# A twelve-pair part of an FFN down projection, computed from 7 block products in place of 8, in a hybrid encoder block on one Trainium2 core

## Chip, core and metric

One core of one Trainium2 chip runs the whole block (1 layer, 512 tokens, model width 2048, all float32). The metric is device time in microseconds of one execution, the median of a few runs.

## What is computed

Cut to what matters here: the second sub-layer, a SwiGLU FFN. Before it the reference runs a token-mixing sub-layer (projections, two attentions, gates, output projection) that the change does not touch.

```python
h = modulate(layer_norm(x), shift2, scale2)          # 512 x 2048
f = (silu(h @ w_ffn_gate) * (h @ w_ffn_up)) @ w_ffn_down   # width 5632, back to 2048
x = layer_norm_affine(DEEPNORM_ALPHA * x + gate2 * f, ln2_g, ln2_b)
```

## The kernel before

Every float32 matrix product is made of three passes of a rounded type: `split` (L94) makes a high part with a ScalarE cast (L97) and a low part with a VectorE subtraction (L98), and `mm3` (L77 to L81) issues high times high, high times low and low times high into one PSUM bank. A weight tile is loaded by SP with `load_raw` (L88, the DMA is L91, 512 KB) into one of 4 buffers named raw, and its two parts into one of 4 buffers each, wh and wl.

The FFN width of 5632 is worked on in 22 pairs of 128 columns. For 20 pairs the gate and up projections already use a 7-product scheme on 2 x 2 blocks (`strassen`, L1069; `weight_sums`, L1051, whose sums run on GpSimd at L1059 to L1061; `combine`, L1087, on VectorE). The hidden activations of a pair, 128 partitions by four blocks of 256 (two halves of the tokens times two column tiles), are multiplied at L1139 and stored to DRAM by `store_hid` (L1016, one DMA on ScalarE's queue).

Then comes the down projection, `down` (L1172): groups of 4 pairs (the fifth group has the rest, and the last 2 pairs are kept for the end). A group loads its hidden blocks (`load_hid`, L1106, SP, with a split at L1110 and L1111), and for each of four 512-wide column chunks takes 4 PSUM banks, one for each 128 tokens; for each pair it loads and splits the 256 x 512 piece of the weight, and issues 4 x 2 x 3 = 24 matmuls of 128x512. `drain` (L1156) then multiplies by gate2 (L1159) and adds to the residual (L1162, L1164), both on VectorE. The last two pairs (L1222 on) have gate2 multiplied into their weights on GpSimd (L1209) and are computed token tile by token tile with the final LayerNorm. In all the down projection is 22 x 96 = 2112 matmuls of 128x512.

A scheduler with a timeline of its own sets the order on every engine; DMAs of one queue start in that order, and an instruction that waits holds up what is behind it on its engine.

```python
for u in range(n):                                              # L1176
    hl = load_split(w_ffn_down, (g0 + u) * 256, 2, cc * 512, 512)
    for t in range(NT):
        for k in range(2):
            mm3(bb[t], hid[u].at(k, t), pair(hl, slice(None), k), u == 0 and k == 0, u == n - 1 and k == 1)
```

Of the kernel before, what the change touches and what calls it, by code (L numbers as in the profile page):

```python
# [46 lines left out]
def block_kernel(ctx: ExitStack, tc: tile.TileContext, x, c, w_ada, b_ada, w_in, b_gates, gqa_q_gain, gqa_k_gain,  # L47
# [1082 lines left out]

    for g in range(N_SPLIT, N_PAIR):
        eg = etile()
        bk = strassen(w_ffn_gate, 2 * g, "ssss")
        combine(eg, bk)
        nc.scalar.activation(out=eg, in_=eg, func=AF.Silu)
        bk = strassen(w_ffn_up, 2 * g, "ggtt", early_hid if g == N_PAIR - 1 else None)
        eu = sw.tile([P, 4, 256], F32, tag="eu", name="eu", bufs=1)
        combine(eu, bk)
        nc.vector.tensor_tensor(out=eg, in0=eg, in1=eu, op=ALU.mult)  # L1139
        store_hid(g, eg)  # L1140
    for u in range(3, GROUP):
        early_hid(u)

    pop("sop", "right")
    xp = push("xp", "right")
    x2 = [xp.tile([P, D], F32, name=f"x3_{t}") for t in range(NT)]
    fw = push("fw", "right")
    gate2 = fw.tile([P, D], F32, name="gate2")

    def load_residual(cc):  # L1150
        cs = slice(cc * 512, (cc + 1) * 512)
        nc.scalar.dma_start(out=gate2[:, cs], in_=rows_d[1][cs].partition_broadcast(P))
        for t in range(NT):
            nc.scalar.dma_start(out=x2[t][:, cs], in_=x2_d[t][:, cs])

    def drain(ps, t, cc, first_):  # L1156
        cs = slice(cc * 512, (cc + 1) * 512)
        tmp = fw.tile([P, 512], F32, tag="tmp", name="dtmp", bufs=3)
        nc.vector.tensor_tensor(out=tmp, in0=ps, in1=gate2[:, cs], op=ALU.mult)  # L1159
        v = x2[t][:, cs]  # L1160
        if first_:
            nc.vector.scalar_tensor_tensor(out=v, in0=v, scalar=ALPHA, in1=tmp, op0=ALU.mult, op1=ALU.add)  # L1162
        else:
            nc.vector.tensor_tensor(out=v, in0=v, in1=tmp, op=ALU.add)  # L1164

    turn8 = [0]

    def dbank():
        turn8[0] += 1
        return bank("ssssgtgt"[(turn8[0] - 1) % 8])  # L1170

    def down(g0, hid, first_, extra=None):  # L1172
        n = len(hid)
        for cc in range(4):
# [1 line left out]
            for u in range(n):  # L1176
                hl = load_split(w_ffn_down, (g0 + u) * 256, 2, cc * 512, 512)
                if first_ and u == 2:
                    load_residual(cc)
                for t in range(NT):  # L1180
                    for k in range(2):
                        mm3(bb[t], hid[u].at(k, t), pair(hl, slice(None), k), u == 0 and k == 0, u == n - 1 and k == 1)
            if extra is not None:
                extra(cc)
            for t in range(NT):
                drain(bb[t], t, cc, first_)

    g0 = 0
    for gi in range(4):
        hid = first_hid if gi == 0 else [load_hid(g0 + i, *hid_slot(4 * (gi % 2) + i)) for i in range(GROUP)]  # L1190
        down(g0, hid, gi == 0)
        g0 += GROUP
    pop("sw", "left")
    hp = push("hp", "left")

    def hp_hid(g):
        return load_hid(g, hp.tile([P, 4, 256], F32R, tag="hh", name="hh", bufs=6), hp.tile([P, 4, 256], F32R, tag="hl", name="hl", bufs=6))
# [5 lines left out]
    wslots = slots(a_pool, "A")[1] + slots(m0, "M")[1]

    def load_last(cc):
        for u in range(N_LAST):
            raw, v = load_raw(w_ffn_down, (gl + u) * 256, 2, cc * 512, 512)
            for k in range(2):
                nc.gpsimd.tensor_tensor(out=v[:, k, :], in0=v[:, k, :], in1=gate2[:, cc * 512:(cc + 1) * 512], op=ALU.mult)  # L1209
                h, l = wslots[cc * 4 + 2 * u + k]  # L1210
                nc.scalar.copy(out=h, in_=v[:, k, :])
                nc.vector.tensor_tensor(out=l, in0=v[:, k, :], in1=h, op=ALU.subtract)
                wl[cc, 2 * u + k] = (h, l)

    down(g0, hid, False, load_last)

    g2 = [hp.tile([P, 512], F32, tag="hh", name="g2", bufs=6) for _ in range(4)]
    b2 = [hp.tile([P, 512], F32, tag="hl", name="b2", bufs=6) for _ in range(4)]
    for j in range(4):
        nc.scalar.dma_start(out=g2[j], in_=ln2_g[0, j * 512:(j + 1) * 512].partition_broadcast(P))  # L1220
        nc.scalar.dma_start(out=b2[j], in_=ln2_b[0, j * 512:(j + 1) * 512].partition_broadcast(P))
# [54 lines left out]
```

## Time and profile before

| | |
|---|---|
| median of 3 runs | 2676.41 us (2674.88 to 2678.2) |
| the profiled execution | 2677.23 us, its span 2675.4 us |
| TensorE busy | 2599.7 us, 97% |
| VectorE, ScalarE, GpSimd busy | 1850.6, 1053.3, 1289.9 us |
| moved by DMA | 456.11 MB, 170 GB/s over the span |
| the down projection's matmuls | from 2185.24 to 2664.15 us of the span |

The span is what the trace covers; the rows are of this one execution. A busy TensorE says that matmuls were in flight, so the number of matmuls in a stretch is the better measure of its pace.

### The profile page before, as it was taken

The page shows a single profiled execution, that of the slowest core. Times are in us where ns is not written, and L with a number is a line of the kernel's source. Part 1 is how long each engine was busy: PE and PEld are TensorE (multiplying, and loading weights), DVE is VectorE, ACT ScalarE, POOL GpSimd, SP SyncE. Part 2 cuts the span into 40 slices and gives each one's busy share as a digit, 9 for nine tenths or more (in the row PEclk, how much of TensorE's full clock was granted, in tenths as well). Part 3 has the DMA queues.
Part 4 walks back from the last instruction along what each step waited for, and adds up shares of the span by engine and source line. Part 5 has one row for each costly group of instructions (what it writes and reads, how often), then busy time and mean ns, then how long its engine had stood idle before and what let it go on. Part 6 is the DMA issues. An engine that isn't in the chain of part 4 may idle for free.

```text
span 2675.4 us, 40191 instructions
## 1 busy us (share of the span) xinstructions
PE 2599.7 (97%) x15563; PEld 2319.2 (87%) x15563; DVE 1850.6 (69%) x2184; ACT 1053.3 (39%) x1525; POOL 1289.9 (48%) x1093
## 2 busy tenths in 40 slices
PE   6999999999989999999899999999999999999998
PEld 5778888788978888887899999999999998888886
DVE  8996688775678644576777777677676655445566
ACT  5542433332344533345644444444444432212321
POOL 4638778785755011021368767777776720000023
PEclk8999999999999999999999999999999999999999
DMA  9977577776744444667763333333333364334442
GB/s 349 295 224 240 165 219 236 241 248 192 212 140 134 127 148 142 225 231 240 229 193 119 115 122 119 118 120 119 111 124 122 111 213 157 115 108 132 150 126 87
DMA packets 330799, 456.11 MB, mean 170 GB/s; under 512 B 19656, under 2 KB 208480, under 8 KB 330096
## 3 DMA queue, kind: packets, MB, share of 16 engines
q1 hardware_dynamic: 307840, 414.77, 49.3%
q10 hardware_dynamic: 22768, 38.78, 4.1%
q8 instruction: 122, 2.00, 0.3%
q14 instruction: 69, 0.57, 0.1%
HBM read 418.87 MB, written 34.62 MB: 170 GB/s over the span
## 4 chain that ended last, share of the span: by engine, by line
PE 83%; POOL 5%; DVE 5%; DMA 3%; issue 2%; ACT 1%; POOLq 0%; SPq 0%; ACTq 0%; DVEq 0%
PE ps_s L81 16%; PE ps_s L80 16%; PE ps_s L79 16%; PE ps_g L80 7%; PE ps_g L79 7%; PE ps_g L81 7%; PE ps_t L80 4%; PE ps_t L79 4%; PE ps_t L81 4%; POOL acc L232 1%; DVE wl L98 1%; DMA braw<-in_w_ada_dram 1%; POOL tmp L228 1%; PE ps_t L584 1%; DVE acc L222 1%
## 5 line engine op out<-in xcount | busy, mean ns | idle before, releaser
L98 DVE TENSOR_TENSOR wl<-raw,wh 128x1024 fp32r<-128x1024 f32 (+2 forms) x342 | 456.9, 1340 | 319.2 <-ACT wh L97 317.6
L97 ACT CAST wh<-raw 128x1024 fp32r<-128x1024 f32 (+2 forms) x342 | 345.8, 1014 | 656.0 <-PE ps_s L81 280.3
L98 DVE TENSOR_TENSOR wl<-tt,wh 128x1024 fp32r<-128x1024 f32 x160 | 237.1, 1482 | 174.9 <-ACT wh L97 174.8
L1059 POOL TENSOR_TENSOR tt<-raw 128x512 f32<-128x512 f32 x160 | 245.8, 1537 | 197.1 <-DMA raw<-in_w_ffn_up_dram 69.5
L232 POOL TENSOR_TENSOR acc<-acc,tmp 128x512 f32<-128x512 f32 (+1 forms) x214 | 297.1, 1389 | 77.1 <-ACT tmp L230 64.6
L97 ACT CAST wh<-tt 128x1024 fp32r<-128x1024 f32 x160 | 167.9, 1049 | 305.9 <-PE ps_s L80 142.8
L1057 DVE TENSOR_TENSOR lr<-raw,hr 128x768 fp32r<-128x768 f32 x160 | 214.8, 1343 | 41.7 <-ACT hr L1056 40.6
L1209 POOL TENSOR_TENSOR raw<-raw,gate 128x512 f32<-128x512 f32 x16 | 25.2, 1600 | 401.0 <-DMA raw<-in_w_ffn_down_dram 400.5
L228 POOL TENSOR_SCALAR tmp<-braw,csil 128x512 f32<-128x512 f32 x112 | 135.4, 1211 | 119.7 <-DMA braw<-in_w_ada_dram 116.6
L1056 ACT CAST hr<-raw 128x768 fp32r<-128x768 f32 x160 | 133.7, 836 | 147.3 <-PE ps_t L80 70.4
L1061 POOL TENSOR_TENSOR tt<-raw,tt 128x256 f32<-128x256 f32 x160 | 173.5, 1085 | 11.9
L1060 POOL TENSOR_TENSOR tt<-raw,tt 128x256 f32<-128x256 f32 x160 | 165.9, 1037 | 11.9
L79 PE MATMUL ps_g<-hTh,wh 128*128 128x512 f32 x384 | 151.8, 396 | 0.0
L81 PE MATMUL ps_g<-hTh,wl 128*128 128x512 f32 x384 | 150.4, 392 | 0.0
L80 PE MATMUL ps_g<-hTl,wh 128*128 128x512 f32 x384 | 150.1, 391 | 0.0
L222 DVE SCALAR_TENSOR_TENSOR acc<-braw,csil,acc 128x512 f32<-128x512 f32 x112 | 113.4, 1012 | 43.3 <-DMA braw<-in_w_ada_dram 42.6
L79 PE MATMUL ps_s<-wh,hTh 128*128 128x512 f32 (+1 forms) x384 | 138.1, 361 | 0.0
L80 PE MATMUL ps_s<-wl,hTh 128*128 128x512 f32 (+1 forms) x384 | 137.5, 358 | 0.0
L81 PE MATMUL ps_s<-wh,hTl 128*128 128x512 f32 (+1 forms) x384 | 137.2, 358 | 0.0
L80 PE MATMUL ps_g<-sl,wh 128*128 128x256 f32 x480 | 135.8, 283 | 0.0
L80 PE MATMUL ps_s<-sl,wh 128*128 128x256 f32 x480 | 135.8, 283 | 0.0
L81 PE MATMUL ps_s<-sh,wl 128*128 128x256 f32 x480 | 135.5, 283 | 0.2 <-DVE wl L98 0.2
(437 smaller groups left out, 8315.2 us busy)
## 6 DMA issues: line engine op xcount, KB each, us to landing
braw<-in_w_ada_dram SPq DMA_DIRECT2D x128, 512.0 KB, 4.2
raw<-in_w_in_dram SPq DMA_DIRECT2D x96, 512.0 KB, 5.0
raw<-in_w_ffn_gate_dram SPq DMA_DIRECT2D x96, 512.0 KB, 3.6
raw<-in_w_ffn_up_dram SPq DMA_DIRECT2D x96, 512.0 KB, 3.6
raw<-in_w_ffn_down_dram SPq DMA_DIRECT2D x88, 512.0 KB, 3.7
raw<-in_w_out_dram SPq DMA_DIRECT2D x64, 512.0 KB, 4.1
lraw<-in_w_ada_dram SPq DMA_DIRECT2D x56, 512.0 KB, 5.5
braw<-in_w_in_dram SPq DMA_DIRECT2D x24, 512.0 KB, 5.2
```

The source lines that it names most:

```text
L79: nc.tensor.matmul(ps, lhsT=ah, rhs=bh, start=start, stop=False)
L80: nc.tensor.matmul(ps, lhsT=ah, rhs=bl, start=False, stop=False)
L81: nc.tensor.matmul(ps, lhsT=al, rhs=bh, start=False, stop=stop)
L97: nc.scalar.copy(out=h[:, :n], in_=src)
L98: nc.vector.tensor_tensor(out=l[:, :n], in0=src, in1=h[:, :n], op=ALU.subtract)
L222: nc.vector.scalar_tensor_tensor(out=acc[:, :n], in0=v[:, k, :], scalar=col, in1=acc[:, :n], op0=ALU.mult, op1=ALU.add)
L228: nc.gpsimd.tensor_scalar(out=dst[:, :n], in0=v[:, k, :], scalar1=col, scalar2=1.0, op0=ALU.mult, op1=ALU.mult)
L232: nc.gpsimd.tensor_tensor(out=acc2[:, :n], in0=acc2[:, :n], in1=dst[:, :n], op=ALU.add)
L1057: nc.vector.tensor_tensor(out=lr, in0=b[:, :, 1:4, :], in1=hr, op=ALU.subtract)
L1059: nc.gpsimd.tensor_tensor(out=t[:, :, 0:2, :], in0=b[:, :, 0:1, :].broadcast_to([P, 2, 2, P]), in1=b[:, :, 1:3, :], op=ALU.subtract)
L1060: nc.gpsimd.tensor_tensor(out=t[:, :, 2, :], in0=b[:, :, 2, :], in1=t[:, :, 0, :], op=ALU.subtract)
L1061: nc.gpsimd.tensor_tensor(out=t[:, :, 3, :], in0=b[:, :, 3, :], in1=t[:, :, 2, :], op=ALU.subtract)
```

## The change

For 12 of the 22 pairs (2 to 13) the product of hidden blocks and weight blocks is made from 7 block products. The 2 x 2 blocks are: token half by column tile of the pair for the activations, column tile of the pair by 1024-column half of the output for the weights. Each of the 7 products is 256 tokens by 128 by 1024. They are made in two sets: set 1 has 3 products, set 2 has 4, and each set runs over the 12 pairs once for each 512-column quarter c of a half. So a pass over one pair (a unit here) is 3 x 2 x 3 = 18 matmuls in set 1 and 24 in set 2, all 128x512.

- Hidden sums (`hidden_sums`): when a pair's activations are ready, four GpSimd operations of 128x256 make the sums, and 6 DMAs on ScalarE's queue store the blocks into `set1_d` and `set2_d` (before: 1 DMA).
- Set tiles: `need1` and `need2` load 384 KB or 512 KB of a pair into a half tile, and split it into one of 12 ring tiles. During the second quarter of set 1 the tile that was used last is handed on to set 2, and in the second quarter of set 2 to the plain pairs.
- Weights: each unit loads its blocks with 2 DMAs on SP (768 KB in set 1, 1024 KB in set 2), adds 256 KB more from DRAM with one accumulating DMA issued by GpSimd, makes 1 (set 1) or 2 (set 2) sums of 128x512 on VectorE, and splits 1536 or 2048 columns. Two half tiles, called a and b here, hold a unit's weights; half tiles are the 4 raw buffers and, once the up projection's tiles are gone, 4 new ones named tp, in turn.
- Results: after each quarter VectorE and ScalarE add the banks into the four token tiles of the sum; set 1 takes 6 banks a quarter, set 2 all 8. `convert` then multiplies by gate2 (GpSimd) and adds the residual, loaded again from DRAM (VectorE, 128x1024).
- The other 10 pairs run as before, in two groups of 4 and the 2 last; their tiles come from the ring and the half tiles.

```diff
+    def hidden_sums(g, eg, e):
+        nc.gpsimd.tensor_tensor(out=e[:, 0], in0=eg[:, 1], in1=eg[:, 2], op=ALU.subtract)
...
+        nc.scalar.dma_start(out=set1_d[g][:, 0:2, :], in_=e[:, 0:2])
+        nc.scalar.dma_start(out=set1_d[g][:, 2, :], in_=eg[:, 3])
+        for b, (t, k) in enumerate(((eg, 0), (e, 2), (eg, 2), (e, 3))):
+            nc.scalar.dma_start(out=set2_d[g][:, b, :], in_=t[:, k])
...
+    def half_tile():
+        place[1] += 1
+        if extra_tiles and place[1] % 2:
+            return extra_tiles[0].tile([P, 1024], F32, tag="tp", name="tp", bufs=4)
+        return raw_tile()
+
+    def load_set(arr, g, n):
+        v = half_tile()[:, :n * 256].rearrange("p (b n) -> p b n", b=n)
+        nc.sync.dma_start(out=v, in_=arr[g])
+        tl = ring_tile((n, g))
+        nc.scalar.copy(out=tl[:, 0:n, 0:256], in_=v)
+        nc.vector.tensor_tensor(out=tl[:, 0:n, 256:512], in0=v, in1=tl[:, 0:n, 0:256], op=ALU.subtract)
+        return tl
...
+    def weights1(g, c):
+        a, b = half_tile(), half_tile()
+        av, bv = a.rearrange("p (b n) -> p b n", b=2), b[:, :512]
+        nc.sync.dma_start(out=av, in_=w_rows(g, 0, c))
+        nc.sync.dma_start(out=bv, in_=w_rows(g, 1, c)[:, 1, :])
+        nc.gpsimd.dma_start(out=av[:, 1], in_=w_rows(g, 0, c)[:, 0, :], accum_op=ALU.add)
+        nc.vector.tensor_tensor(out=bv, in0=bv, in1=av[:, 1], op=ALU.add)
+        ah, al = split(a, 1024)
+        bh, bl = split(bv, 512)
+        return ((2, (ah[:, :512], al[:, :512])), (1, (bh[:, :512], bl[:, :512])), (0, (ah[:, 512:], al[:, 512:])))
+
+    def weights2(g, c):
...
+        nc.sync.dma_start(out=bv, in_=w_rows(g, 0, c))
+        nc.sync.dma_start(out=av, in_=w_rows(g, 1, c))
+        nc.gpsimd.dma_start(out=bv[:, 1], in_=w_rows(g, 1, c)[:, 1, :], accum_op=ALU.add)
+        nc.vector.tensor_tensor(out=bv[:, 0], in0=bv[:, 0], in1=av[:, 0], op=ALU.add)
+        nc.vector.tensor_tensor(out=bv[:, 0], in0=bv[:, 0], in1=bv[:, 1], op=ALU.add)
+        ah, al = split(a, 1024)
+        bh, bl = split(b, 1024)
...
+    def products(pairs, sets, weights, c, step):
+        bk = None
+        for u, g in enumerate(pairs):
+            ws = weights(g, c)
+            if bk is None:
+                bk = [dbank() for _ in range(2 * len(ws))]
+            step(u, False)
+            for j, (b, w) in enumerate(ws):
+                for i in range(2):
+                    mm3(bk[2 * j + i], block(sets[g], b, i), w, u == 0, u == len(pairs) - 1)
+            step(u, True)
+        return bk
...
+            for i in range(2):
+                add(nc.vector, z(0, 1, i, c), bk[i])
+            for i in range(2):
+                add(nc.vector, z(0, 0, i, c), bk[2 + i])
+            for i in range(2):
+                add(nc.vector, z(1, 0, i, c), bk[4 + i])
+                nc.vector.tensor_tensor(out=z(1, 1, i, c), in0=z(1, 1, i, c), in1=bk[4 + i], op=ALU.subtract)
+            for i in range(2):
+                add(nc.vector, z(1, 0, i, c), bk[6 + i])
```

How the built program's order moves, at two places. First SP's queue, the loads of the down projection. A group of the kernel before, hidden blocks of 4 pairs and then 16 weight pieces (L91):

```order
L1109 DMA raw<-hid_d 128x1024 x4
L91 DMA raw<-in_w_ffn_down_dram 128x2x512 x16
L1109 DMA raw<-hid_d 128x1024 x4
L91 DMA raw<-in_w_ffn_down_dram 128x2x512 x16
L1109 DMA raw<-hid_d 128x1024 x4
```

Some units of set 1, second quarter, in the changed program (L1203 loads a, L1204 b, L1129 is the set tile for set 2):

```order
L1129 DMA tp<-set_d 128x1024
L1204 DMA tp<-in_w_ffn_down_dram 128x512
L1203 DMA raw<-in_w_ffn_down_dram 128x2x512
L1129 DMA raw<-set_d 128x1024
L1204 DMA raw<-in_w_ffn_down_dram 128x512
L1203 DMA tp<-in_w_ffn_down_dram 128x2x512
L1129 DMA tp<-set_d 128x1024
L1204 DMA tp<-in_w_ffn_down_dram 128x512
L1203 DMA raw<-in_w_ffn_down_dram 128x2x512
```

Where a queue had one load for 24 matmuls, it now has three for 18, and raw and tp take turns.

Second VectorE, at the seam between the last up projection and the down projection. Before (L1090 to L1093 are `combine` of the last pair, L1139 its product):

```order
L98 TENSOR_TENSOR wl_22373<-raw_22370,wh_22372 128x1024
L98 TENSOR_TENSOR wl_22403<-raw_22400,wh_22402 128x1024
L98 TENSOR_TENSOR wl_22433<-raw_22430,wh_22432 128x1024
L1090 TENSOR_TENSOR eu_22342<-ps_g_22098,eu_22342 128x512
L1091 TENSOR_TENSOR eu_22342<-ps_g_22099,eu_22342 128x512
L1092 TENSOR_TENSOR eu_22342<-ps_g_22099,eu_22342 128x256
L1093 TENSOR_TENSOR eu_22342<-ps_t_22100,eu_22342 128x512
L1139 TENSOR_TENSOR eg_21863<-eg_21863,eu_22342 128x1024
```

In the changed program (L1206 is the sum in set 1, L1132 a set tile's low part, L1092 to L1095 and L1170 the same `combine` and product):

```order
L98 TENSOR_TENSOR wl_22482<-raw_22475,wh_22481 128x1024
L1132 TENSOR_TENSOR Ml0_22571<-raw_22569,Ml0_22571 128x3x256
L1092 TENSOR_TENSOR eu_22451<-ps_g_22208,eu_22451 128x512
L1093 TENSOR_TENSOR eu_22451<-ps_g_22209,eu_22451 128x512
L1094 TENSOR_TENSOR eu_22451<-ps_g_22209,eu_22451 128x256
L1206 TENSOR_TENSOR tp_22476<-tp_22476,raw_22475 128x512
L1095 TENSOR_TENSOR eu_22451<-ps_t_22210,eu_22451 128x512
L1170 TENSOR_TENSOR eg_21973<-eg_21973,eu_22451 128x1024
L98 TENSOR_TENSOR wl_22486<-tp_22476,wh_22485 128x512
L1132 TENSOR_TENSOR Mh0_22534<-tp_22532,Mh0_22534 128x3x256
L1206 TENSOR_TENSOR tp_22556<-tp_22556,raw_22555 128x512
```

Before, three weight pieces were split ahead of the seam. Now one half tile of the first unit (raw_22475) is, and its other half tile, tp_22476, lies in memory that the up projection's matmuls read to their end; SP's load into it waits for TensorE.

## Rows read from the trace of the kernel before

**Rows 1.** The page's part 1, busy time of each engine, share, instructions:

```profile
PE 2599.7 (97%) x15563; PEld 2319.2 (87%) x15563; DVE 1850.6 (69%) x2184; ACT 1053.3 (39%) x1525; POOL 1289.9 (48%) x1093
```

**Rows 2.** The page's part 2: granted clock (PEclk) in 40 slices:

```profile
PEclk8999999999999999999999999999999999999999
```

**Rows 3.** Busy time by stretch: us, busy us (instructions), granted clock, DMA share, GB/s:

```profile
core 0: us, PE busy (x) PEld busy (x) DVE busy (x) ACT busy (x) POOL busy (x), PEclk, DMA share, GB/s
...
2060.00:2140.00 80.00, 80.00 (x670) 80.00 (x669) 58.28 (x50) 32.92 (x38) 57.29 (x49) 1.00 0.38 119
2200.00:2300.00 100.00, 100.00 (x443) 82.81 (x442) 51.44 (x63) 24.01 (x24) 0.00 (x0) 1.00 0.47 157
2300.00:2400.00 100.00, 100.00 (x443) 82.81 (x442) 46.99 (x56) 23.64 (x23) 0.00 (x0) 1.00 0.37 117
```

**Rows 4.** TensorE's timeline, first and last matmul of the stage: start us, us:

```profile
2185.24 0.40 PE L79 MATMUL ps_s<-wh,Ah 128*128 128x512 f32 x1
...
2663.76 0.39 PE L81 MATMUL ps_t<-Mh,hl 128*128 128x512 f32 x1
```

**Rows 5.** VectorE and ScalarE, lines by shape, 2180 to 2676 us: busy, mean ns:

```profile
L98 DVE TENSOR_TENSOR wl<-raw,wh 128x1024 fp32r<-128x1024 f32 x80 | 100.6, 1260 | 150.6 <-ACT wh L97 150.5
L1164 DVE TENSOR_TENSOR x<-x,dtmp 128x512 f32<-128x512 f32 x64 | 42.0, 681 | 0.1
...
L1111 DVE TENSOR_TENSOR Ml<-raw,Mh 128x1024 fp32r<-128x1024 f32 x8 | 9.8, 1220 | 15.6 <-ACT Mh L1110 15.6
...
L97 ACT CAST wh<-raw 128x1024 fp32r<-128x1024 f32 x79 | 83.0, 1053 | 239.8 <-PE ps_t L81 128.5 <-PE ps_s L81 87.9 <-DMA x<-x_d 16.1
...
L1211 ACT CAST Mh<-raw 128x512 fp32r<-128x512 f32 x8 | 5.0, 622 | 11.3 <-POOL raw L1209 11.3
```

**Rows 6.** Two rows of VectorE and ScalarE in the gate and up projections, timeline:

```profile
1715.26 0.96 DVE L1057 TENSOR_TENSOR lr<-raw,hr 128x768 fp32r<-128x768 f32 x1 [0.71 <-ACT hr L1056]
...
1708.85 0.33 ACTq L1017 DMA_DIRECT2D hid_d<-eg  x1
1709.35 0.84 ACT L1056 CAST hr<-raw 128x768 fp32r<-128x768 f32 x1 [1.10 <-PE ps_s L80]
```

**Rows 7.** SP's waits, 2180 to 2640 us: queue line <- releaser: us, times, longest:

```profile
SPq L91 <- DVE wl L98: 246.9, 67, 5.8
```

**Rows 8.** The trace's DMA issues by line: KB each, median us to landing:

```profile
raw<-in_w_ffn_down_dram SPq DMA_DIRECT2D x88, 512.0 KB, 3.7
...
lraw<-in_w_ada_dram SPq DMA_DIRECT2D x56, 512.0 KB, 5.5
...
raw<-hid_d SPq DMA_DIRECT2D x22, 512.0 KB, 4.6
...
x<-x_d ACTq DMA_DIRECT2D x16, 256.0 KB, 8.2
out_dram<-x SPq DMA_DIRECT2D x16, 256.0 KB, 2.1
...
yt<-yg_d SPq DMA_DIRECT2D x8, 256.0 KB, 4.6
```

**Rows 9.** Stretch of densest loads: its windows row, then its DMA issues:

```profile
40.00:60.00 20.00, 17.75 (x76) 14.56 (x74) 19.65 (x20) 10.28 (x14) 11.02 (x7) 0.92 1.06 375
...
lraw<-in_w_ada_dram SPq DMA_DIRECT2D x8, 512.0 KB, 7.7
```

**Rows 10.** GpSimd's lines in the gate and up projections: busy, mean ns:

```profile
L1061 POOL TENSOR_TENSOR tt<-raw,tt 128x256 f32<-128x256 f32 x160 | 173.5, 1085 | 11.9
L1060 POOL TENSOR_TENSOR tt<-raw,tt 128x256 f32<-128x256 f32 x160 | 165.9, 1037 | 11.9
```

**Rows 11.** Busy time by stretch, as in Rows 3: around a stall of TensorE:

```profile
96.00:100.00 4.00, 1.80 (x8) 1.14 (x7) 4.00 (x3) 1.47 (x2) 3.37 (x2) 1.00 0.83 225
100.00:104.00 4.00, 3.41 (x14) 2.96 (x15) 3.93 (x8) 0.26 (x1) 0.00 (x0) 0.66 0.96 331
104.00:108.00 4.00, 4.00 (x18) 3.27 (x17) 3.87 (x6) 4.00 (x7) 0.94 (x1) 0.91 1.02 350
```

More of the change, by code (lines that the diff above doesn't have):

```diff
@@ new lines, in block_kernel, with early @@
+    first = GROUPS[0]
+    def early(u):
+        need1(first[u])
+    for g in range(N_SPLIT, N_PAIR):
+        eg = etile()
+        bk = strassen(w_ffn_gate, 2 * g, "ssss")
+        combine(eg, bk)
+        nc.scalar.activation(out=eg, in_=eg, func=AF.Silu)
+        bk = strassen(w_ffn_up, 2 * g, "ggtt", early if g == N_PAIR - 1 else None)
+        eu = sw.tile([P, 4, 256], F32, tag="eu", name="eu", bufs=1)
+        combine(eu, bk)
+        nc.vector.tensor_tensor(out=eg, in0=eg, in1=eu, op=ALU.mult)
+        if g in by_sums:
+            hidden_sums(g, eg, eu)
+        else:
+            store_hid(g, eg)
@@ new lines, in tmp_tile, with add, convert @@
+    def tmp_tile():
+        return fw.tile([P, 512], F32, tag="tmp", name="dtmp", bufs=3)
+    def add(eng, v, ps):
+        eng.tensor_tensor(out=v, in0=ps, in1=v, op=ALU.add)
+    def convert(c, ts=range(NT)):
+        for t in ts:
+            zv = quad(x2[t], c)
+            xc = half_tile().rearrange("p (b n) -> p b n", b=2)
+            nc.sync.dma_start(out=xc, in_=quad(x2_d[t], c))
+            nc.gpsimd.tensor_tensor(out=zv, in0=zv, in1=quad(gate2, c), op=ALU.mult)
+            nc.vector.scalar_tensor_tensor(out=zv, in0=xc, scalar=ALPHA, in1=zv, op0=ALU.mult, op1=ALU.add)
@@ L1131, in block_kernel @@
[L1131 to L1174, printed above, removed]
+        plain_hid[g] = Hid(h, l)
+    def down(pairs, cols, following):
+        following = list(following)
+        for n, cc in enumerate(cols):
+            cs = slice(cc * 512, (cc + 1) * 512)
             bb = [dbank() for _ in range(NT)]
[L1176 to L1179, printed above, removed]
+            for u, g in enumerate(pairs):
+                hl = load_split(w_ffn_down, g * 256, 2, cc * 512, 512)
@@ L1185, in down @@
             for t in range(NT):
[L1186 to L1197, printed above, removed]
+                tmp = tmp_tile()
@@ L1199, in block_kernel @@
+                nc.vector.tensor_tensor(out=tmp, in0=bb[t], in1=gate2[:, cs], op=ALU.mult)
+                add(nc.vector, x2[t][:, cs], tmp)
+        return following
     gl = N_PAIR - N_LAST
-    hid = [hp_hid(g) for g in range(g0, gl)]
-    hid_l = [hp_hid(gl + i) for i in range(N_LAST)]
     wl = {}
[L1203 to L1207, printed above, removed]
-            for k in range(2):
[L1209 to L1221, printed above, removed]
+    def load_last(cc, u):
+        def fn():
+            raw, v = load_raw(w_ffn_down, (gl + u) * 256, 2, cc * 512, 512, half_tile)
+            tl = ring_tile(("w", cc, u))
+            nc.gpsimd.tensor_tensor(out=v, in0=v, in1=gate2[:, cc * 512:(cc + 1) * 512].unsqueeze(1).broadcast_to([P, 2, 512]), op=ALU.mult)
+            nc.scalar.copy(out=tl[:, 0:2, :], in_=v)
+            nc.vector.tensor_tensor(out=tl[:, 2:4, :], in0=v, in1=tl[:, 0:2, :], op=ALU.subtract)
+            for k in range(2):
+                wl[cc, 2 * u + k] = (tl[:, k, :], tl[:, 2 + k, :])
+        return fn
@@ new lines, in block_kernel @@
+    for gi in range(len(GROUPS)):
+        if gi + 1 < len(GROUPS):
+            left = strassen_down(gi, [lambda g=g: need1(g) for g in GROUPS[gi + 1]])
+            assert not left
+        else:
+            spare = len(RING) - len(GROUPS[gi])
+            for f in queue[:spare]:
+                tick(f)
+            queue = strassen_down(gi, queue[spare:])
+    if PLAIN:
+        convert(1)
+        for grp in PLAIN:
+            queue = down(grp, (0, 2, 1, 3), queue)
+    while later:
+        f = later.pop(0)
+        if f is not None:
+            f()
@@ L1222, in block_kernel @@
+    for f in queue:
+        f()
+    if not PLAIN:
+        convert(1)
     for t in range(NT):
```

150 lines of the change are left out of this document (130 added, 20 removed).

## Prediction

> **What bounds the kernel now.** I read the page's busy times first: TensorE has matmuls in flight for 97% of the span [rows 1], and the granted clock stands at its upper level, 2.4 GHz, in every slice but the first [rows 2]. So the span is close to a count of matmuls. Then I read the stretches: in the down projection 443 matmuls of 128x512 go through in 100 us, 0.2257 us each, without a gap, while VectorE is busy for 47% of it, ScalarE for 24%, GpSimd not at all, and the DMA engines for 37% at 117 GB/s [rows 3]. The 2112 matmuls of the stage run from 2185.24 to 2664.15 us [rows 4]. One matmul less there is worth 0.2257 us as long as its operands come in time. They do so by a wide margin today: SP's queue stood 246.9 us waiting for VectorE to free a raw buffer [rows 7]; the loads wait for the consumer.
>
> **What is removed.** 12 pairs x 96 matmuls become 12 x 84. 144 x 0.2257 = **32.5 us**. No wait eats into it today, so all of it counts.
>
> **Work per unit against TensorE's time.** A unit of set 1 takes TensorE 18 x 0.2257 = 4.06 us, one of set 2 24 x 0.2257 = 5.42 us. VectorE, set 1: one sum of 128x512 (0.68), low parts of 1024 (1.26) and 512 columns (0.68, the price of the other operation of that size), 2.62 in all [rows 5]; a set tile adds 0.96 (768 columns [rows 6]) or 1.22 (1024 [rows 5]). At most 3.84 of 4.06. Set 2: 2 x 0.68 + 2 x 1.26 = 3.88, with a tile for the plain pairs 5.10, of 5.42. ScalarE: casts of 1.05 and 0.62, and 0.84 or 1.05 for the tile, 2.7 of 4.06 [rows 5, 6]. The cover that the stage has today is gone; what is left of the 32.5 us depends on five terms.
>
> **Term B, the seam at the start.** The first unit's tile b can be loaded only when the up projection's last matmuls have gone. Landing 3.7 us [rows 8], sum 0.68, cast 0.62: 5.0 us. TensorE has 12 matmuls on tile a meanwhile, 2.7 us, and waits 2.3. The second unit's a is loaded behind the seam too and needs the accumulating DMA. No row has one. The nearest are plain DMAs of 256 KB: 2.1 us (the stores of the output), 4.6 (yt, a plain load of stored activations) and 8.2 (x_d, 16 in a burst) [rows 8]. I take 4.6, as it is an isolated load like these. Then a is cast at 3.7 + 4.6 + 1.05 = 9.4 us; TensorE is free at 5.0 + 6 x 0.2257 = 6.4 and waits 3.0. In the trace a 4-us stretch with 1.80 us of matmuls is followed by stretches at a granted clock of 0.66 and 0.91 [rows 11], 4 x 0.34 + 4 x 0.09 = 1.7 us lost. Sum **7 us**; 3 if the accumulate takes 2.1, 11 if it takes 8.2.
>
> **Term C, set 1: how long a half tile is held.** There are 8 half tiles, and a unit of set 1 uses three: a, b and the set tile. So eight tiles serve 8/3 units, and the unit can't be shorter than the sum of its three holds divided by 8. A load lands after 3.7 us at today's rate, after 7.7 in the densest stretch at 375 GB/s, after 5.5 in the median of all lraw loads, of which that stretch has the slowest [rows 8, 9]. At 4.4 us per unit the stage would move 1.44 to 1.57 MB (1024 KB of weights and a set of 384 or 512 KB) in that time, 328 to 357 GB/s, so I take 5.5. Hold of a: 5.5 + accumulate 4.6 + cast 1.05 + low part 1.26 + 1.0 behind other work = 13.4. Hold of b: 5.5 + 4.6 + sum 0.68 + cast 0.62 + low part 0.68 + 1.0 = 13.1. Set tile: 5.5 + 0.9 + 1.0 + 1.0 = 8.4. Together 34.9, by 8: 4.36 us, 0.3 over TensorE's 4.06. 24 units: **+8 us** with rounding. From below, with 3.7 and 2.1, the holds give 24.5 / 8 = 3.1, and nothing is lost; from above, with 7.7 and 8.2, 48.7 / 8 = 6.1, and 49 us are lost. This is the term that decides.
>
> A page of the Trainium skill prices the DMA that I could only bound: "DMA: Bandwidth & Descriptors", section "Anatomy of one DMA — SWDGE (gpsimd) path", gives a DMA issued by GpSimd about 2.0 us plus its bytes at 436 GB/s, which makes an estimate of 2.6 us for 256 KB. By it the three holds would be 30.9, term C nothing, and the time about 2658 us. No row of this trace shows one.
>
> **Term D, set 2's second quarter.** VectorE has 12 x 3.88, nine tiles for the plain pairs (11.0), ten sums out of the banks of the quarter before (6.8) and four residual sums of 128x1024 (at 1.26, 5.0): 69.4 us against TensorE's 12 x 5.42 = 65.0. **+4 us**; 0 if the first quarter's slack (53 of 65 us) carries over in the two units of wh and wl that are ready ahead, 14 if the residual loads take 8.2 us once [rows 8] and low parts lengthen.
>
> **Term E, banks at the seams.** Set 2 uses all 8 banks. Its last unit closes two banks every 1.35 us and VectorE empties two in 1.36, so it keeps pace unless weights stand between. 1 us at each of two seams, **+2** (0 to 6).
>
> **Term F, gate and up projections.** Four GpSimd sums of about 1.06 us [rows 10] add 4.2 us to a pair of 16 x 21 matmuls x 0.1194 = 40 us (670 in 80 us). GpSimd is busy for 72% there [rows 3] and would be for 83%. ScalarE issues five DMAs more, 5 x 0.33 [rows 6]. Tiles are ready one to two units of 5 us ahead, which hides it: **+1** (0 to 10). The last two pairs, the LayerNorm and the output stay as they are: 0. The 8 multiplications by gate2 run on a GpSimd that is idle today: 0.
>
> **Sum.** 7 + 8 + 4 + 2 + 1 = 22 against 32.5: 10.5 us won. The profiled execution took 2677.2 us, which makes 2666.7; the median of the runs stands 0.8 lower, so **2666 us**.
>
> **Rivals.**
> 1. *The accumulating DMA lengthens the holds (slower).* Mechanism: a waits for its load, then for GpSimd's DMA, and b's sum waits for that. The place is set 1. It decides from the point where C reaches 32.5 - 14 = 18.5 us, a unit of 4.83 us, holds of 38.6 instead of 34.9: an accumulate of 6.5 us instead of 4.6 does it, since both a and b hold for it. At 8.2 us the holds are 42.1, the unit 5.26, C 29 and B 11: 2666 + 21 + 4 = 2691 us. For it: 256 KB in a crowd did take 8.2 [rows 8]. Against: GpSimd has nothing else to do there, and yt took 4.6. Chance 0.27.
> 2. *Everything hides.* With the lower ends, B 3 and the rest 2 to 3, the time is 2677.2 - 32.5 + 5 - 0.8 = 2649 us. For it: SP's 246.9 us of waiting shows how far ahead the loads can be [rows 7]. Chance 0.17.
> 3. *The accumulate's bytes count twice.* If a DMA engine has to read the tile as well as the weight, a unit of set 1 moves 1.70 or 1.84 MB, at 375 GB/s [rows 9] 4.54 or 4.89 us; 9 units each lose 0.14 and 0.49 more than in my sum, 6 us: 2672 us. No row tells for or against it; that the loads run far below 375 GB/s today says only that there is room. Chance 0.14. The Trainium skill, "DMA: Bandwidth & Descriptors", section "Rules for kernel authors", says that an accumulate reads its destination and writes it later, which speaks for this rival.
> 4. *The clock falls with the gaps.* If set 1's lost time comes in gaps of 2.2 us as at 96 us [rows 11], seven of them cost 7 x 1.7 = 12 us more: 2678 us. Against it: gaps of 0.3 us per unit are far from that. Chance 0.05. The Trainium skill, "TensorE: Matmul & The Clock Gate", Part 1, says that the array drops to the lower level after idling and returns after sustained work; the trace agrees with 0.66 after the gap.
>
> That the matmuls stay can be ruled out: TensorE's order has 144 rows fewer.
>
> **How the numbers follow.** My own case has 0.37, with a range of its own of 2657 to 2675. The range for 8 in 10 runs from 2650 (half of rival 2 lies below) to 2693 (nearly half of rival 1 above). A measurement of this kernel can tell 0.2%, 5.4 us, from no change: faster is under 2671.0, slower over 2681.8. Faster: 0.29 of my case, 0.17 of rival 2, which is 0.46. Same: 0.08 of my case, 0.14 of rival 3, 0.01 of rival 1: 0.23. Slower: 0.26 of rival 1 and 0.05 of rival 4, which could lie beyond its 2678: 0.31.
>
> **What would show it.** The matmuls of 128x512 fall by 144. GpSimd's accumulating DMA has a row: 4.6 us to landing confirms the sum, 2.6 makes it too high, 6.5 or more brings rival 1. 24 units of set 1 take 24 x 4.36 = 105 us. TensorE waits for ScalarE's wh and VectorE's wl, some 20 us in all, in set 1 and in the second half of set 2, and not in the gate and up projections. VectorE is over 85% busy there. I am wrong if set 1 takes over 116 us, or if TensorE waits before the seam.

## The result and the profile after

The changed kernel takes **2737.4 us** (median of 4 runs, 2733.2 to 2742.1) where the kernel before, beside it on the same chip, takes 2677.3 (4 runs, 2674.9 to 2679.9): ratio 1.0224, 95% interval 1.0209 to 1.0238. It is 60 us slower; the forecast was 2666, in a range up to 2693. The profiled execution of the changed kernel has a span of 2731.5 us, that of the kernel before 2675.4.

From the page of the changed kernel, the busy time of the engines, the granted clock in 40 slices, and two DMA queues (packets, MB, share of 16 engines' span):

```profile
PE 2593.1 (95%) x15419; PEld 2301.4 (84%) x15419; DVE 1916.5 (70%) x2248; ACT 1101.6 (40%) x1585; POOL 1457.0 (53%) x1189
...
PEclk8999999999999999999999999999999989999999
...
q1 hardware_dynamic: 322880, 444.66, 51.5%
...
q0 software_dynamic: 6912, 12.59, 2.7%
```

The 144 matmuls are gone (15563 in [rows 1], 15419 here), and PE's busy time fell by 6.6 us only. The last slices show nothing alarming, because a slice of the page is 68 us long and mixes stages. The stretches of the down projection do show it. Same view as [rows 3], cut where set 1's two column halves, set 2's two, and the plain pairs with the last begin and end:

```profile
core 0: us, PE busy (x) PEld busy (x) DVE busy (x) ACT busy (x) POOL busy (x), PEclk, DMA share, GB/s
...
2184.00:2262.00 78.00, 55.68 (x208) 42.61 (x209) 39.98 (x50) 26.70 (x35) 11.33 (x13) 0.85 0.87 237
2262.00:2339.00 77.00, 59.40 (x220) 45.78 (x220) 44.44 (x52) 32.96 (x41) 10.44 (x12) 0.87 0.85 251
2339.00:2410.00 71.00, 65.88 (x287) 53.25 (x285) 47.76 (x55) 27.03 (x28) 10.52 (x13) 1.00 0.83 232
2410.00:2490.00 80.00, 70.85 (x291) 55.96 (x292) 68.81 (x71) 31.25 (x31) 21.22 (x14) 0.96 0.88 276
2490.00:2720.00 230.00, 219.87 (x959) 181.13 (x957) 147.18 (x161) 50.22 (x52) 55.29 (x30) 0.98 0.33 105
```

In [rows 3] 443 matmuls filled 100 us. Here 208 and 220 take 78 and 77, with VectorE busy for 40 and 44, ScalarE for 27 and 33, GpSimd for 11. **None of these engines is full in set 1: everyone waits.** The DMA engines have transfers in flight for 87 and 85% of the time, but move 237 and 251 GB/s, where [rows 9] have 375.

I count the stage's matmuls in the trace, from the start of the first to the end of the 432nd (set 1), of the 1008th (set 2) and of the last. All 1968 are there. The times of sets and quarters below are counted in this way. "At full pace" is the count by 0.2257 us:

| us | at full pace | changed kernel | lost | forecast to be lost |
|---|---|---|---|---|
| set 1 | 97.5 | 156.6 | 59.1 | 15 (B 7, C 8) |
| set 2 | 130.0 | 151.8 | 21.8 | 6 (D 4, E 2) |
| plain pairs and the last two | 216.7 | 230.7 | 14.0 | 0 |

The stage starts at 2181.26 us, 4 us earlier than before [rows 4], and lasts 539.1 us instead of 478.9: it loses 94.9, where the stage before lost 2.2, and gains 32.5.

What TensorE waits for in set 1, 2180 to 2339 us (queue, line, releaser: us, times, longest):

```profile
PE ps_s L80 <- DVE wl L98: 15.4, 6, 5.6
PE ps_s L79 <- ACT wh L97: 10.5, 2, 5.5
PE ps_t L80 <- DVE wl L98: 9.7, 3, 4.2
PE ps_t L79 <- ACT wh L97: 4.2, 2, 2.5
```

These are 39.8 us of the 59.1. The other 19 or so are no waits: 84 of the 432 matmuls start 0.43 us in the mean after the one before, instead of 0.2257, with no releaser. They ran at the lower clock. The granted clock was 0.85 and 0.87 in the two halves, and 0.50, the lower level of 1.2 GHz, in the worst ten microseconds, after waits:

```profile
2190.00:2200.00 10.00, 4.01 (x8) 2.29 (x9) 5.07 (x7) 2.95 (x5) 1.75 (x2) 0.50 1.00 283
```

How long the transfers take in set 1, 2183 to 2322 us (as in [rows 8]: issues, KB each, median us to landing; those of POOLq are the accumulates):

```profile
tp<-in_w_ffn_down_dram SPq DMA_DIRECT2D x17, 512.0 KB, 7.3
raw<-in_w_ffn_down_dram SPq DMA_DIRECT2D x8, 512.0 KB, 6.1
tp<-in_w_ffn_down_dram POOLq DMA_DIRECT2D x15, 256.0 KB, 6.9
...
raw<-in_w_ffn_down_dram POOLq DMA_DIRECT2D x7, 256.0 KB, 5.4
```

The forecast had 5.5 for a load and 4.6 for an accumulate.

One pair of set 1 shows where a half tile's time goes. Rows of four timelines, in order SP, POOL, DVE, ACT (start, us, what, [idle before, what ended it]):

```profile
2288.70 0.33 SPq L1204 DMA_DIRECT2D raw<-in_w_ffn_down_dram  x1
2289.30 0.55 SPq L1203 DMA_DIRECT2D tp<-in_w_ffn_down_dram  x1
2290.44 0.33 SPq L1129 DMA_DIRECT2D tp<-set_d  x1
...
2292.18 0.55 SPq L1203 DMA_DIRECT2D raw<-in_w_ffn_down_dram  x1
...
2303.35 0.55 SPq L1203 DMA_DIRECT2D tp<-in_w_ffn_down_dram  x1
...
2294.77 0.88 POOL L1205 DMA_DIRECT2D tp<-in_w_ffn_down_dram  x1 [9.47 <-DMA tp<-in_w_ffn_down_dram]
...
2301.49 0.69 DVE L1206 TENSOR_TENSOR raw<-raw,tp 128x512 f32<-128x512 f32 x1 [6.30 <-DMA tp<-in_w_ffn_down_dram]
2302.10 1.22 DVE L1132 TENSOR_TENSOR Mh<-tp,Mh 128x1024 fp32r<-128x1024 f32 x1
2303.24 1.82 DVE L98 TENSOR_TENSOR wl<-tp,wh 128x512 fp32r<-128x512 f32 x2
...
2295.59 1.05 ACT L1131 CAST Mh<-tp 128x1024 fp32r<-128x1024 f32 x1 [1.66 <-DMA tp<-set_d]
2301.62 1.05 ACT L97 CAST wh<-tp 128x1024 fp32r<-128x1024 f32 x1 [4.47 <-DMA tp<-in_w_ffn_down_dram]
```

Tile a's load is issued at 2289.30, its accumulate at 2294.77, and only at 2301.5 can b's sum and a's cast run. Two landings stand in series: 5.5 us, then 6.7. The set tile, loaded at 2290.44, is cast at 2295.59, but its low part runs at 2302.10: VectorE works in order and **stands at b's sum for 6.30 us with the set tile's low part behind it**. So tiles that need no accumulate are held by it too. The set tile, forecast at 8.4 us, is held for 2303.3 - 2290.4 = 12.9. SP, which needs a free tile, issues the next pair's L1203 at 2292.18, and then none before 2303.35: two pairs in 14.05 us, for which TensorE needs 8.1.

### The profile page after: what moved, and what is told of

The parts are those of the page before. It is cut to its first block, busy times and chain, and to the rows that moved or that the text cites. A ratio compares the mean times of both kernels' runs of the same rounds, so it can differ in the third digit from the quotient of the medians.

```text
span 2731.5 us, 40540 instructions
## 1 busy us (share of the span) xinstructions
PE 2593.1 (95%) x15419; PEld 2301.4 (84%) x15419; DVE 1916.5 (70%) x2248; ACT 1101.6 (40%) x1585; POOL 1457.0 (53%) x1189
## 4 chain that ended last, share of the span: by engine, by line
PE 71%; DMA 9%; DVE 8%; POOL 5%; issue 4%; ACT 2%; POOLq 0%; SPq 0%; ACTq 0%; DVEq 0%
PE ps_s L80 15%; PE ps_s L81 15%; PE ps_s L79 15%; PE ps_g L80 6%; PE ps_g L79 6%; PE ps_g L81 6%; DMA tp<-in_w_ffn_down_dram 4%; DVE wl L98 3%; PE ps_t L80 3%; PE ps_t L81 3%; PE ps_t L79 2%; DMA raw<-in_w_ffn_down_dram 2%; POOL acc L234 1%; DMA braw<-in_w_ada_dram 1%; DVE acc L224 1%
## 5 line engine op out<-in xcount | busy, mean ns | idle before, releaser
L97 ACT CAST wh<-raw 128x1024 fp32r<-128x1024 f32 (+2 forms) x342 | 338.8, 995 | 593.9 <-PE ps_s L81 238.8
L98 DVE TENSOR_TENSOR wl<-tt,wh 128x1024 fp32r<-128x1024 f32 x160 | 230.3, 1439 | 192.8 <-ACT wh L97 190.5
L1059 DVE TENSOR_TENSOR lr<-raw,hr 128x768 fp32r<-128x768 f32 x160 | 205.8, 1286 | 43.6 <-ACT hr L1058 42.4
L1063 POOL TENSOR_TENSOR tt<-raw,tt 128x256 f32<-128x256 f32 x160 | 199.2, 1246 | 11.8
L1062 POOL TENSOR_TENSOR tt<-raw,tt 128x256 f32<-128x256 f32 x160 | 198.2, 1239 | 11.0
L79 PE MATMUL ps_g<-hTh,wh 128*128 128x512 f32 x384 | 151.8, 396 | 0.0
L81 PE MATMUL ps_g<-sh,wl 128*128 128x256 f32 x480 | 135.6, 282 | 0.0
```

What stands on the lines that cost most here:

```text
L79: nc.tensor.matmul(ps, lhsT=ah, rhs=bh, start=start, stop=False)
L81: nc.tensor.matmul(ps, lhsT=al, rhs=bh, start=False, stop=stop)
L97: nc.scalar.copy(out=h[:, :n], in_=src)
L98: nc.vector.tensor_tensor(out=l[:, :n], in0=src, in1=h[:, :n], op=ALU.subtract)
L1059: nc.vector.tensor_tensor(out=lr, in0=b[:, :, 1:4, :], in1=hr, op=ALU.subtract)
L1062: nc.gpsimd.tensor_tensor(out=t[:, :, 2, :], in0=b[:, :, 2, :], in1=t[:, :, 0, :], op=ALU.subtract)
```

## The experiments

Three explanations are tested. Theory 1: the accumulate puts a second landing on the way of a half tile, and eight tiles can't cover it. Theory 2: its bytes take throughput from the loads. Theory 3: VectorE, with its added sums, is the bound. Diffs are against the changed kernel unless said otherwise.

**The sum without a transfer.** The block that the accumulate fetches from memory lies in a half tile already, and VectorE can add it from there.

```diff
# e1 (both sets), e10 (weights1 only); e4: nc.gpsimd
-        nc.gpsimd.dma_start(out=av[:, 1], in_=w_rows(g, 0, c)[:, 0, :], accum_op=ALU.add)
+        nc.vector.tensor_tensor(out=av[:, 1], in0=av[:, 1], in1=av[:, 0], op=ALU.add)
-        nc.gpsimd.dma_start(out=bv[:, 1], in_=w_rows(g, 1, c)[:, 1, :], accum_op=ALU.add)
+        nc.vector.tensor_tensor(out=bv[:, 1], in0=bv[:, 1], in1=av[:, 1], op=ALU.add)
```

> The two accumulating transfers of a pair are replaced by additions on VectorE (the added block lies in SBUF already); all else stays as in the changed kernel, 2737 us. Theory 1 (the accumulate's 6.4 us landing lengthens the time for which a half tile is held, and all engines wait for it): set 1 falls from 155.8 us to 100-115 us, set 2's second quarter is bound by VectorE (about 77 us), and the whole comes to about 2680 us (2670 to 2692). Theory 2 (the accumulates take DMA throughput away from the loads of the same stretch): also about 2680 us, since the transfers are gone. Theory 3 (VectorE's additions are the bound): 48 more additions of about 0.7 us make it slower, 2745 us or more.

Measured: 2686.8 us, 1.0038 (1.0026 to 1.0050) of the kernel before: **50.6 us of the 60 are gone**, although VectorE has 48 additions more. Theory 3 falls. Set 1 takes 108.9 us instead of 156.6. The stretches and the 512 KB loads there:

```profile
2190.00:2250.00 60.00, 56.57 (x235) 46.10 (x236) 53.17 (x72) 31.77 (x41) 0.00 (x0) 0.92 0.80 266
2250.00:2290.00 40.00, 39.98 (x177) 32.81 (x176) 36.48 (x45) 24.14 (x28) 0.00 (x0) 1.00 0.90 296
```

```profile
tp<-in_w_ffn_down_dram SPq DMA_DIRECT2D x25, 512.0 KB, 5.0
```

177 matmuls in 40 us are full pace, the clock is back, and the plain loads alone move 296 GB/s, more than loads and accumulates together did.

**The same bytes, off the way.** e1 with the accumulates added to two tiles that nobody reads.

```diff
 # against e1, in weights1 and likewise in weights2; dtmp has 1 buffer instead of 3
+        nc.gpsimd.dma_start(out=junk[place[0] % 2], in_=w_rows(g, 0, c)[:, 0, :], accum_op=ALU.add)
+        place[0] += 1
```

> As e1_add_on_vector, and the same accumulating transfers of the same 256 KB run too, but into two tiles that nobody reads (one tile of the converts' three is given up for room). Theory 1 (the hold): within 8 us of e1_add_on_vector, since nothing waits for the landing. Theory 2 (DMA throughput): 2715 us or more, near the changed kernel, with loads of 512 KB still landing in about 7 us in set 1; in e1_add_on_vector they land in 5.5 us or less.

Measured: 2696.1 us, 9.3 above e1, a little more than Theory 1 allowed and 19 below what Theory 2 needs. Its rows for the same stretches and landings:

```profile
2190.00:2250.00 60.00, 53.63 (x225) 42.72 (x226) 50.12 (x66) 29.13 (x38) 13.88 (x16) 0.94 1.08 324
2250.00:2290.00 40.00, 38.49 (x168) 30.85 (x167) 34.55 (x42) 21.51 (x26) 9.59 (x11) 1.00 1.06 324
```

```profile
tp<-in_w_ffn_down_dram SPq DMA_DIRECT2D x23, 512.0 KB, 7.6
junk<-in_w_ffn_down_dram POOLq DMA_DIRECT2D x38, 256.0 KB, 6.8
raw<-in_w_ffn_down_dram SPq DMA_DIRECT2D x14, 512.0 KB, 9.9
```

Here loads land as late as in the changed kernel or later (7.6 and 9.9 us), with 324 GB/s moved, and set 1 takes 113.7 us, 4.8 more than in e1. Late loads alone hurt little: eight tiles cover one landing of that length. The smaller buffer for dtmp has no part in it: the plain pairs, which use it, take 228.8 us against 228.4. So about 9 of 50 us are the bytes, and the rest is the place of the accumulate in the chain.

**Which set, and which engine.**

> Only set 1's accumulating transfer is replaced by an addition on VectorE; set 2 keeps its accumulates. Theory 1 (the hold of the half tiles, which decides in set 1, where three of them turn over per 4.06 us of matmuls): nearly all of the gain of e1_add_on_vector, 2737 - 47 = 2690 us (2684 to 2698). If the accumulates cost the same per transfer in both sets, half of that gain is lost: about 2712 us.

Measured: 2702.7 us, 34.7 below the changed kernel: between the two forecasts, and outside the range of Theory 1. Set 1 takes 107.9, but set 2, untouched, takes 164.6 where it took 151.8 behind the slow set 1, all of it in its first quarter (85.2 us instead of 72.3). So my figure of 47 misses by what set 2 gives back when it is reached at nearly full pace; why it does was not tried. Against e1 set 2's own accumulates cost 2702.7 - 2686.8 = 15.9 us.

> The two accumulating transfers of a pair are replaced by GpSimd additions of about 1.05 us on the same engine that issued them for 0.87 us. Theory 1: about 2675 us (2662 to 2692): the hold loses 5 us per half tile and VectorE gets no more instructions. Theory 2: the same. Theory 3 (VectorE is the bound): 2730 us or more, since VectorE's work is that of the changed kernel.

Measured: 2704.7 us, 1.0113 (1.0095 to 1.0130): 17.9 worse than on VectorE, outside what I expected. Set 1 takes 116.1, set 2 164.1 us (108.9 and 150.8 in e1). VectorE and GpSimd in e4 between 2305 and 2390 us, then VectorE in e1, columns as in [rows 5]:

```profile
L98 DVE TENSOR_TENSOR wl<-raw,wh 128x1024 fp32r<-128x1024 f32 x13 | 25.6, 1972 | 0.0
L98 DVE TENSOR_TENSOR wl<-tp,wh 128x1024 fp32r<-128x1024 f32 x13 | 19.1, 1467 | 0.0
...
L1216 POOL TENSOR_TENSOR raw<-raw,tp 128x512 f32<-128x512 f32 x12 | 20.7, 1724 | 51.9 <-DMA raw<-in_w_ffn_down_dram 34.5 <-DMA tp<-in_w_ffn_down_dram 8.6 <-DVE raw L1217 5.8
```

```profile
L98 DVE TENSOR_TENSOR wl<-raw,wh 128x1024 fp32r<-128x1024 f32 x14 | 18.7, 1335 | 0.8 <-ACT wh L97 0.8
L98 DVE TENSOR_TENSOR wl<-tp,wh 128x1024 fp32r<-128x1024 f32 x13 | 15.9, 1221 | 1.0 <-ACT wh L97 1.0
```

A GpSimd addition took 1.72 us; the 1.05 expected is the price of half its columns [rows 10]. VectorE's low part took 1.97 and 1.47 us in the mean, for raw and tp, where e1 has 1.34 and 1.22. VectorE is slower beside GpSimd, so work moved to GpSimd is paid on VectorE as well. That this makes up all of the 17.9 us is not shown.

**More half tiles.**

```diff
 # e11; e15 has (place[1] + 1) % 9; dtmp has 1 buffer instead of 3
-        if extra_tiles and place[1] % 2:
-            return extra_tiles[0].tile([P, 1024], F32, tag="tp", name="tp", bufs=4)
+        if extra_tiles and place[1] % 9 % 2 == 0:
+            return extra_tiles[0].tile([P, 1024], F32, tag="tp", name="tp", bufs=5)
```

> The changed kernel, accumulates and all, with nine half tiles instead of eight in the down stage (five of tp, four of raw; two tiles of the converts' three are given up for room). Theory 1 (hold): the unit of set 1 goes from 6.45 us to 6.45 x 8/9 = 5.73 us, 24 units, so up to 17 us less: 2720 us (2712 to 2728). Theory 2 (DMA throughput) and theory 3 (VectorE): 2737 us within 5.

Measured: 2731.2 us, 6 less, which settles nothing by itself: set 1 fell to 128.8 us from first to last matmul, but began behind a wait of 15.0 us, since the first pair's a went into a tp tile, free only after the up projection.

> As e11_nine_half_tiles (the changed kernel with its accumulates and nine half tiles), with the rotation shifted so that set 1's first block again goes into a raw tile, which is free before the tp tiles are; in e11_nine_half_tiles that seam took 15 us while set 1 itself, first to last matmul, fell from 157.5 to 128.7 us. Theory 1 (hold): without the seam's loss 2709 us (2702 to 2716). Theory 2 (DMA throughput) and theory 3 (VectorE): 2731 us or more.

Measured: 2725.0 us, 12.4 less, between the two forecasts. Set 1 took 133.5 us instead of 156.6, and starts on time: **one tile more gave 23.1 us there**, as Theory 1 has it and neither rival. Set 2 took 162.7 instead of 151.8 and gave half of it back, as in e10.

**Second landing, or accumulating?**

```diff
 # e20, against e1, before each sum: the second block loaded again
+        nc.gpsimd.dma_start(out=av[:, 1], in_=w_rows(g, 0, c)[:, 1, :])
 # e19, against e1: the load split over two queues
-        nc.sync.dma_start(out=av, in_=w_rows(g, 0, c))
+        nc.sync.dma_start(out=av[:, 0], in_=w_rows(g, 0, c)[:, 0, :])
+        nc.gpsimd.dma_start(out=av[:, 1], in_=w_rows(g, 0, c)[:, 1, :])
```

> e1_add_on_vector with a plain 256 KB transfer on GpSimd's queue, issued where the accumulate stood: it loads the same block again into the same half tile after the first load has landed, and VectorE adds as in e1_add_on_vector. The bytes from memory are those of the changed kernel. If a second landing in series is the cost: 2715 to 2745 us, the changed kernel's. If it is the accumulating (the engine's reading and adding in SBUF): 2700 us or less.

> e1_add_on_vector, where one 256 KB block of every 512 KB load goes through GpSimd's software queue as a plain transfer, beside the other half and not behind it. If what costs in the changed kernel is a second landing in series on the way of a half tile: within 12 us of e1_add_on_vector (2687 us), since no landing stands behind another. If the software queue's transfers themselves cost (GpSimd's 0.87 us for each issue, their slow packets): 2715 us or more.

Measured: e20 2728.9 us, 1.0192 (1.0177 to 1.0208); e19 2683.3 us, 1.0022 (1.0012 to 1.0032). GpSimd's transfers in set 1, 2183 to 2322 us, of e20 and of e19, and the page's line of their queue (packets, MB, share of 16 engines' span):

```profile
tp<-in_w_ffn_down_dram POOLq DMA_DIRECT2D x16, 256.0 KB, 4.3
...
raw<-in_w_ffn_down_dram POOLq DMA_DIRECT2D x9, 256.0 KB, 5.1
...
q0 software_dynamic: 3840, 12.59, 1.4%
```

```profile
tp<-in_w_ffn_down_dram POOLq DMA_DIRECT2D x17, 256.0 KB, 5.0
...
raw<-in_w_ffn_down_dram POOLq DMA_DIRECT2D x13, 256.0 KB, 4.6
...
q0 software_dynamic: 3840, 12.59, 1.3%
```

The same queue, size and about the same landing: in series the plain transfer costs 42 us against e1, beside the load it costs nothing. e20 also moves 256 KB more a pair than e1, for which e2 allows about 9 us; the other 33 are the series. **The cost is mainly a second landing in series, of whatever kind.** The changed kernel, whose accumulates land after 6.9 and 5.4 us instead of 4.3 and 5.1, takes 8.4 us more than e20. Two things lie in this chain, the half tiles held longer and VectorE standing at b's sum; e15 shows that the tiles count, and no run changes VectorE's order alone.

The Trainium skill, "DMA: Bandwidth & Descriptors", section "Anatomy of one DMA — SWDGE (gpsimd) path", gives a DMA issued by GpSimd about 2.0 us plus its bytes at 436 GB/s, an estimate of 2.6 us for 256 KB. The rows here, with loads on the other queue beside it, have 4.3 to 5.1 us in the median, and the measurement decides.

**The seam into the plain pairs.** In the changed kernel TensorE waits once for 9.0 us behind set 2, when both engines are at convert(1):

```profile
2500.00:2520.00 20.00, 13.87 (x49) 10.95 (x50) 20.00 (x8) 4.51 (x5) 17.19 (x6) 0.75 0.50 156
```

VectorE is busy for all of the 20 us with 8 instructions, four of them converts and four low parts of weights. e5 spreads the converts over the first plain pairs:

```diff
+                if n == 1 and g in PLAIN[0]:
+                    convert(1, [u])
 # in down's loop; and before it:
-        convert(1)
```

> The changed kernel with one edit: the eight GpSimd and VectorE instructions that scale the second column half between set 2 and the plain pairs are spread over the first four plain pairs. If the 9.0 us stall of TensorE after set 2 comes from VectorE being busy with them (20.0 of 20.0 us in that stretch), the time falls by 8 to 14 us to about 2727 us. If it comes from the accumulates of set 2 landing late, it stays within 3 us of 2737 us. The other theories say nothing on it.

Measured: 2726.4 us, 11 less, as expected.

**Towards a better version.** On top of e1:

```diff
 # e12, in down's loop; convert(0, ...) out of set 2, convert(1) out from ahead of the plain pairs
+                if n < 2 and g in PLAIN[0]:
+                    convert(n, [u])
 # e13 as well: two sums of weights2 in one
+        nc.vector.tensor_tensor(out=b, in0=b, in1=a, op=ALU.add)
 # e16 as well: converts with PLAIN[1]; the first four plain pairs add ungated
+                if pairs is PLAIN[0]:
+                    add(nc.vector, x2[t][:, cs], bb[t])
+                    continue
 # e17: e16 with nine half tiles, raw tiles for both blocks of the first pair; e18: e17 with the accumulates
```

> e1_add_on_vector with both converts spread over the first four plain pairs (the first column half's in their first pass, the second's in their second), so that set 2's second quarter has no GpSimd multiplication and no convert on VectorE. If what is left there is VectorE being full (74.95 of 79 us, its additions at 1.05 to 1.11 us beside GpSimd and 0.69 without): the seam gives 9 to 11 us as in e5_late_convert, the quarter 6 to 9 us, and it comes to 2669 us (2663 to 2676), below the kernel before. If the quarter waits for transfers: 2677 us.

> e12_vector_late_converts with set 2's two additions of 512 columns on the same pair of tiles (0.69 us each) made one of 1024 columns (about 1.22 us): 24 x 0.16 = 4 us less on VectorE. If VectorE still sets set 2's pace, 2 to 4 us below e12_vector_late_converts; if not, within 2 us of it.

Measured: 2675.5 and 2674.9 us, both not to be told from the kernel before (0.9995, 0.9986 to 1.0004; 0.9994, 0.9986 to 1.0003), and from each other. The first lies between its two forecasts, 2669 and 2677, and the second did not bring the 2 to 4 us that VectorE as the limit would have given. The traces of e13 and of the next kernel, e16, tell more. The stretch of set 2's second quarter in each, and TensorE's wait at its end in e13:

```profile
2373.00:2450.00 77.00, 69.73 (x290) 56.80 (x290) 74.23 (x66) 36.41 (x36) 19.15 (x8) 0.92 0.75 252
...
PE ps_g L79 <- DVE x L1251: 7.3, 1, 7.3
```

```profile
2366.00:2433.00 67.00, 66.91 (x288) 55.24 (x289) 63.75 (x61) 33.83 (x33) 8.63 (x3) 0.97 0.78 258
```

In e13 GpSimd still has 8 instructions there, 6 of them of the converts: moved in the source, the converts were ordered ahead again.

> e13_vector_late_fused, where the order of the instructions had put the converts into set 2's second quarter again (8 GpSimd multiplications, VectorE 74.2 of 77 us there). Now the first four plain pairs add their banks without the gate (one addition in the place of a multiplication and an addition), and the converts come after them, so they can't be moved ahead. If VectorE sets set 2's pace: the second quarter falls from 77 to about 68 us, 2664 us in all (2658 to 2670). If not: 2674 us within 3.

Measured: 2666.7 us, 0.9968 (0.9955 to 0.9980): faster than the kernel before. Made to depend on the first plain pairs, the converts stay behind. From its first matmul to its last the quarter took 72 us in e13 and takes 71 here, for 65.0 at full pace; what went is the 7.3 us for which TensorE waited behind it for VectorE to empty a bank (L1251). Just before that sum e13 has two converts of 1.2 us on VectorE and two low parts of 3.4 us each, beside two GpSimd multiplications for the last pairs. How much of the wait is the converts' is not shown; e16 also leaves out 16 multiplications of the plain pairs.

> e16_vector_convert_after with nine half tiles and a raw tile for both blocks of set 1's first pair. Set 1 takes 113.8 us in e13_vector_late_fused where its matmuls need 97.5 us. Theory 1: the hold still costs there even without the accumulate, 5 to 12 us less than e16_vector_convert_after, about 2657 us. Theory 3: within 3 us of e16_vector_convert_after.

Measured: **2663.9 us, 0.9956 (0.9943 to 0.9968) of the kernel before, the lowest median of the study**, but only 2.8 below e16, whose interval overlaps, so it is Theory 3's number, not mine: set 1 takes 110.1 us with nine tiles and 109.1 with eight. Without the accumulate, eight tiles suffice.

> e17_nine_tiles_vector with the two accumulating transfers put back in the place of the VectorE additions. Theory 1: nine tiles pay back some half of the accumulates' cost, so 20 to 40 us slower than e17_nine_tiles_vector, about 2690 us. Theory 3: VectorE has 48 additions fewer, so no slower than e17_nine_tiles_vector.

Measured: 2712.7 us, 48.8 above e17: the accumulates cost as much in the repaired kernel as in the changed one, more than I expected of nine tiles. They do so at other places. Set 1 is 30.3 us longer than in e17, 24.3 of it in its first quarter, with one wait of 14.3 us at the start, and 5.9 in its second, where the changed kernel is 26.6 longer than e1. Set 2 is 18.5 longer, where the changed kernel is 1.0 longer than e1. So with the ninth tile the accumulates cost less in set 1's second quarter and more in set 2; why was not tried.

## Why the prediction was wrong

- **Removed work: right.** 144 matmuls went, and where the operands come in time they go at the pace of before (177 in 40 us in e1).
- **Term C is the step that failed.** The mechanism, half tiles held for two landings, was right, and its size was wrong: 8 us forecast, where B and C together lost 59.1, as much as both upper ends (11 and 49). A pair of set 1's second quarter took 75.9 / 12 = 6.32 us, not 4.36, and more than the 6.1 of my upper end. Four parts of it were mis-sized. The accumulate landed in 6.9 and 5.4 us instead of 4.6, and the loads in 6.1 to 7.3 instead of 5.5. The holds were taken tile by tile, as if a tile waited for its own transfers only; but VectorE works in order, and at b's sum it kept the set tile as well (12.9 us instead of 8.4). And I gave the clock no part, where about 19 us went.
- **Rival 1 was the right one, and priced too low.** It decides from 6.5 us for the accumulate, it said; the tp accumulates landed in 6.9. At 8.2 it put the time at 2691. The runs show that the landing's length is not what matters most: e20's second landing took 4.3 to 5.1 us, near my 4.6, and still cost 42 us, some 9 of them for the bytes. With the right length for the accumulate, the sum would still have been wrong.
- **Rival 4 came along with it.** I gave the clock 12 us and a chance of 0.05; with rival 1 true, the waits came in gaps of 2 to 6 us, and about 19 us went at a granted clock of 0.85 and 0.87. The two should not have been priced as separate cases: the first brings the second.
- **Rival 3 (bytes) has a small part:** 9.3 us in e2, where 6 were forecast. What its mechanism would do is seen too: the accumulates kept the DMA engines for 2.7% of the span, as many plain bytes on the same queue for 1.3 to 1.4% (e19, e20).
- **Term B:** the two waits at the start are the row of 10.5 us for ScalarE's wh, both before 2206 us, where I had 2.3 and 3.0; and the clock of 0.50 behind them cost some 4 us up to 2206, not the 1.7 that I took from [rows 11].
- **Terms D and E, 6 us, measured 21.8** in set 2, 14.5 of it in the second quarter and 7.3 in the first, for which I had at most E's 2; 14.0 more went at the plain pairs. VectorE's work in the second quarter was right (69.4 us forecast, 68.8 measured). I let the residual sums count at 1.26 us each and GpSimd's multiplications beside them at nothing, because GpSimd is idle there today. Beside each other they took longer: 8 instructions filled VectorE's 20 us at 2500. e5 shows 11 us for the second convert, and e16 against e13 8.2 for the converts' place together with the multiplications left out.
- **Term F: right.** The gate and up projections did not get longer; the stage behind them began 4 us earlier.
- Of the signs that I named, "wrong if set 1 takes over 116 us" came true with 156.6.

## What to carry to other kernels

Count the landings in series on the way of a buffer, not the bytes: a DMA that waited for another DMA put a tile's last landing at 12.2 us instead of 5.5 in the pair shown, and VectorE, which works in order and stood at the result, held the buffers of others too. Before a sum is given to an accumulating transfer, look whether both addends are on the chip already: an addition of 0.69 us on VectorE in each of 48 units saved 50 us of the kernel here, although VectorE was the busier engine. Work put on an idle GpSimd was not free while VectorE was busy beside it.
